# Feed-forward of a two-layer decoder: operand sums of the down projection formed beside gate and up, and its first product taken in native fp32

## The chip, the cores and the metric

One core of a Trainium2 chip runs the whole program. The metric is the device time of one execution in microseconds (us). Before the change it is 2813.67 us, the median of three runs (2801.68 to 2820.46).

## What is computed

Two decoder layers on 1024 tokens of width 1024. Each is an attention block followed by a feed-forward block; the change touches only the second.

```python
def swiglu(h, w_gate, w_up, w_down):
    return (jax.nn.silu(h @ w_gate) * (h @ w_up)) @ w_down
...
        x = x + swiglu(rms_norm(x, f_norm), w_gate, w_up, w_down)
```

The inner width D_FF is 2816, which is 22 blocks of 128. All data are float32, transposed: a tile has 128 features on the partitions and 512 tokens (half of the sequence) in the free dimension.

## The kernel before, in words

**A pair.** The function `pair` (L252) computes two blocks of output features for both halves of the tokens, that is four results of 128x512. It does so as a 2x2 block product with seven multiplications in place of eight. Four weight blocks A11, A12, A21, A22 are loaded into `raw` tiles, four sums S1 to S4 of them are formed on GpSimd (POOL, `gadd`, L163), and on the other side stand seven operands made of the activations: X11, X21, X22 and four sums, T1 to T4 (T4 and its like are made in `xadds`, L231; T3 overwrites X12). Products have numbers 1 to 7 and are issued in the order 1, 6, 5, 7, 2, 4, 3 (`ORDER`, L28). Product 1 is A11 times X11 alone.

**A split.** Each operand is used as a rounded high part and a low part (`split`, L152): ScalarE (ACT) writes the high part, VectorE (DVE) subtracts it from the source and writes the low part. One product over one block k is then three matmuls, high times high and the two mixed ones (L288). A weight operand is split once for each pair, into a `wo` tile; an activation operand once for each chunk, into an `xo` tile (ring `b4`, 28 tiles, of which five hold running sums during the down projection).

**Gate and up.** `ffn` (L1145) runs eleven iterations i. Each has a gate pair and an up pair with four blocks k, 84 matmuls a pair. The evacuation `fu` (L1169) of the up pair multiplies the up result into the stored gate result: a DVE instruction adds bank and a partial sum, a POOL instruction multiplies; only for the result (0, 0) DVE multiplies directly. Each of the four 128x512 results is stored to `hS` in DRAM (L1177).

**Down.** Here the inner width is worked through in four chunks of 3, 3, 3 and 2 blocks k (`DOWN`, L27). For each k of a chunk `hadds` (L1152) loads two rows of `hS`, 512 KB each, and forms T1 to T4 on POOL; then seven operands are split. The first two k of the first chunk are fetched during the last gate and up pairs (`PRE`, L37). A chunk has four pairs p. The pair p = 0 goes through `kmajor` (L335): seven banks are open at once, and all seven products are done for one k before the next k, so it can start when the first k is split. Its evacuation `f` (L1213) has a POOL add and a DVE add for two thirds of the results. The pairs p = 1 to 3 go product by product and add each bank into the running sums as soon as it is complete (`plus`, L295), nine DVE adds a pair.

**What sets the order.** A scheduler orders the instructions of each engine when the program is built, from its own estimate of times; on the chip each engine then works through its list in that order. All loads and stores stand in one list, on the SP queue.

Of the kernel before, what the change touches and what calls it, by code (L numbers as in the profile page):

```python
# [9 lines left out]
F32 = mybir.dt.float32  # L10
# [23 lines left out]
LAG = 12  # L34
RLAG = 7
MOFF = 56
PRE = 2  # L37
FGT = 7
LATE = (0,)
PESQ = (0, 16)  # L40
# [87 lines left out]
class Trunk:  # L128
# [120 lines left out]
            X[n, i] = t  # L249
            self.split(t[:, 0], t[:, 1], s)  # L250

    def pair(self, w, nk, X, evac, first=None, acc=None):  # L252
        nc = self.nc
        raw = []
        for b in range(4):
# [15 lines left out]
        A = {}  # L271
        src = {1: A11, 6: S2, 5: S1, 7: S3, 2: A12, 4: A22, 3: S4}
        for n in ORDER:
            t = self.tl("hl" if first and n in ORDER[5:] else "wo", "wo", (P, 2, 4, P), F32R)
            self.split(t[:, 0, 0:nk], t[:, 1, 0:nk], src[n], -1.0 if n == 4 else 1.0)
            A[n] = t
# [7 lines left out]

        def prod(n, bank, first):
            m = 0
            for k in range(nk):
                for a, b in ((0, 0), (0, 1), (1, 0)):  # L288
                    nc.tensor.matmul(bank, A[n][:, a, k], X[n, k][:, b], start=first and m == 0,  # L289
                                     stop=m == 3 * nk - 1, skip_group_check=True)  # L290
                    m += 1
# [852 lines left out]

    def ffn(self, l, e, src, dst, nxt):  # L1145
        nc, I = self.nc, self.I
        hS = self.dr.tile([22, P, T], F32, name=f"hS{l}")
        X, rs = e["X"], e["rs"]
        wg, wu = I[f"w{l}g"], I[f"w{l}u"]
        early = []  # L1150

        def hadds(i):  # L1152
            q = []
            for k in (2 * i, 2 * i + 1):
                t = self.hl("hld", dt=F32)
                self.load(t.rearrange("p a b -> p (a b)"), hS[k])
                q.append((t[:, 0], t[:, 1]))
            return self.xadds(*q)
        for i in range(11):
            s2 = {}  # L1160

            def fg(ti, hf, bank, add):
                c = self.tl("C", "s")
                self.emul(c, bank, add, rs[hf])
                nc.scalar.activation(c, c, AF.Silu)
                self.gadd(c, c, rs[hf], ALU.mult)
                s2[ti, hf] = c

            def fu(ti, hf, bank, add):  # L1169
                s = s2[ti, hf]  # L1170
                if add is None:
                    nc.vector.tensor_tensor(s, bank, s, ALU.mult)
                else:
                    u = self.tl("T", "u")
                    nc.vector.tensor_tensor(u, bank, add, ALU.add)
                    self.gadd(s, s, u, ALU.mult)
                nc.sync.dma_start(hS[2 * i + ti, :, hf * H:(hf + 1) * H], s)  # L1177
            self.pair(wg[i], 4, X, fg, first=i == 0 and (0, 1, 2, 3))
            if i == 10:
                for k in range(PRE):  # L1180
                    early.append(hadds(k))
            self.pair(wu[i], 4, X, fu)
        acc = {}
        base = 0
        for c, nk in enumerate(DOWN):
            X = {}
            for i in range(nk):
                self.xsplit(X, i, early.pop(0) if early else hadds(base + i))
            end = c == len(DOWN) - 1
            for p in range(4):  # L1190
                got = {}

                def place(ti, hf):
                    return slice((p + 4 * ti) * P, (p + 4 * ti + 1) * P), slice(hf * H, (hf + 1) * H)

                def start(ti, hf):
                    key = (p, ti, hf)
                    if c == 0:
                        if p == 0 or (p == 1 and ti == 0):
                            acc[key] = self.tl("C", "acc")  # L1200
                        else:
                            if (p, ti, 1 - hf) not in acc:
                                acc[p, ti] = self.tl("b4", "acc2", (P, 2, H))
                            acc[key] = acc[p, ti][:, hf]
                        self.load(acc[key], src[place(ti, hf)])
                    return acc[key]

                def done(ti, hf, r):
                    if end:
                        nc.sync.dma_start(dst[place(ti, hf)], r)  # L1210
                        got[ti, hf] = r

                def f(ti, hf, bank, add):  # L1213
                    r = start(ti, hf)
                    if add is not None:
                        self.gadd(r, r, add, ALU.add)
                    nc.vector.tensor_tensor(r, bank, r, ALU.add)
                    done(ti, hf, r)
                if p == 0:
                    self.pair(I[f"w{l}d{c}"][p], nk, X, f, first=tuple(range(nk)))  # L1220
                else:
                    self.pair(I[f"w{l}d{c}"][p], nk, X, done, acc=start)
                if end and nxt is not None:
                    self.absorb(nxt, p, [[got[t, h] for h in range(2)] for t in range(2)], "hl")
            base += nk
# [140 lines left out]
```

## Time and profile before

| | |
|---|---|
| median of three runs | 2813.67 us |
| the profiled execution, its own time | 2817.3 us |
| its span, first to last instruction | 2815.5 us |
| gate and up of the second layer, even stretch | about 2150 to 2549 us |
| down of the second layer | about 2549 to 2815.5 us |
| down of the first layer | about 1175 to 1475 us, its end beside the next layer's input projection |

Times inside the span are counted from its start. PE is the matmul engine, PEld its weight loads. A busy PE row says that matmuls were in flight; their ends are modelled, so the spacing of starts is the measure of throughput. The names in a row are output<-inputs; "x" with a number is how many instructions a row holds, and what stands after "<-" in brackets is what ended the idle time before it.

### The profile page before, as it was taken

How to read it: one execution, taken by the hardware profiler on the slowest of the kernel's cores; microseconds unless marked ns; L12 is line 12 of the kernel's file. 1: busy time of each engine (PE TensorE's matmuls, PEld its weight loads, DVE VectorE, ACT ScalarE, POOL GpSimd, SP SyncE). 2: the span in 40 equal slices, each digit the busy share in tenths (PEclk: the TensorE clock that was granted, in tenths of full speed). 3: DMA queues.
4: the chain of work that ended last, by engine and by line, in shares of the span. 5: the costliest groups of instructions: out<-in, count | busy, mean ns of one | idle time of the engine just before them, and what ended most of it. 6: DMA issues, size and time to landing. Idle time of an engine off the chain costs nothing.

```text
span 2815.5 us, 35148 instructions
## 1 busy us (share of the span) xinstructions
PE 2622.2 (93%) x11422; PEld 1963.0 (70%) x11422; DVE 2179.3 (77%) x3063; ACT 1367.4 (49%) x2640; POOL 1587.7 (56%) x1355
## 2 busy tenths in 40 slices
PE   7999998997899999998999998999789999998889
PEld 3775554765678888776758866666567888886667
DVE  8777777886965555788899887999799555558987
ACT  5437775673533332343367753777544333333333
POOL 5545665135576666876565533122556666678763
PEclk9999997998999999999999999999899999999999
DMA  3466645624232222242233437666242322224222
GB/s 116 162 203 196 197 148 151 160 84 143 86 98 89 85 77 86 89 149 87 76 109 125 144 123 223 151 176 181 94 133 67 108 86 75 86 77 163 90 90 90
DMA packets 166511, 343.38 MB, mean 122 GB/s; under 512 B 20524, under 2 KB 43904, under 8 KB 166328
## 3 DMA queue, kind: packets, MB, share of 16 engines
q1 hardware_dynamic: 160888, 329.21, 37.9%
q0 software_dynamic: 5056, 11.84, 1.4%
q8 instruction: 90, 1.47, 0.2%
q14 instruction: 93, 0.76, 0.1%
q10 hardware_dynamic: 384, 0.10, 0.0%
HBM read 232.96 MB, written 108.09 MB: 121 GB/s over the span
## 4 chain that ended last, share of the span: by engine, by line
PE 63%; DVE 17%; issue 5%; ACT 5%; DMA 4%; POOL 2%; SPq 0%; DVEq 0%; ACTq 0%; POOLq 0%
PE bb L289 19%; PE bc L289 13%; PE ba L289 13%; PE O L995 5%; DVE xo L156 5%; PE St L974 4%; PE P L342 3%; DVE wo L156 3%; PE Sm L948 2%; DVE acc L298 1%; DVE R L1079 1%; DVE p L985 1%; ACT xo L155 1%; PE psu L659 1%; PE Sz L1069 1%
## 5 line engine op out<-in xcount | busy, mean ns | idle before, releaser
L289 PE MATMUL bb<-xo,wo 128*128 128x512 f32 x2970 | 746.8, 398 | 13.0 <-DVE U L323 4.6
L289 PEld LDWEIGHTS bb<-xo,wo 128*128 128x128 f32 x2970 | 560.9, 190 | 155.3 <-DVE U L323 6.6
L289 PE MATMUL ba<-xo,wo 128*128 128x512 f32 x1980 | 518.6, 406 | 38.3 <-DVE acc L298 19.8
L289 PE MATMUL bc<-xo,wo 128*128 128x512 f32 x1980 | 499.3, 398 | 11.9 <-ACT sq L409 9.4
L289 PEld LDWEIGHTS ba<-xo,wo 128*128 128x128 f32 x1980 | 381.8, 194 | 140.2 <-issue 19.1
L289 PEld LDWEIGHTS bc<-xo,wo 128*128 128x128 f32 x1980 | 373.0, 189 | 107.8 <-ACT sq L409 10.2
L155 ACT ACTIVATE wo<-S 128x512 fp32r<-128x512 f32 (+2 forms) x416 | 241.5, 586 | 413.0 <-PE bb L289 128.4
L156 DVE TENSOR_TENSOR wo<-S,wo 128x512 fp32r<-128x512 f32 (+2 forms) x416 | 381.0, 919 | 72.8 <-ACT wo L155 71.4
L165 POOL TENSOR_TENSOR S<-raw 128x512 f32<-128x512 f32 (+2 forms) x208 | 292.3, 1406 | 111.8 <-DVE wo L156 93.5
L342 PE MATMUL P<-xo,wo 128*128 128x512 f32 x966 | 270.6, 425 | 67.9 <-DVE xo L156 26.0
L995 PE MATMUL O<-p,v 128*65 128x512 f32 (+3 forms) x1152 | 302.4, 364 | 7.9 <-ACT p L984 4.2
L342 PEld LDWEIGHTS P<-xo,wo 128*128 128x128 f32 x966 | 189.7, 202 | 142.5 <-DVE xo L156 39.4
L165 POOL TENSOR_TENSOR S<-raw,S 128x512 f32<-128x512 f32 (+2 forms) x104 | 133.2, 1281 | 272.6 <-issue 153.8
L165 POOL TENSOR_TENSOR s<-s,rs 128x512 f32<-128x512 f32 x156 | 234.5, 1512 | 76.5 <-DVE wo L156 45.3
L155 ACT ACTIVATE wo<-raw 128x512 fp32r<-128x512 f32 (+2 forms) x208 | 121.8, 586 | 312.3 <-PE bb L289 187.4
L156 DVE TENSOR_TENSOR wo<-raw,wo 128x512 fp32r<-128x512 f32 (+2 forms) x208 | 197.8, 951 | 34.0 <-ACT wo L155 34.0
L995 PEld LDWEIGHTS O<-p,v 128*65 128x65 f32 x1152 | 146.9, 142 | 71.5 <-ACT p L155 11.0
L985 DVE TENSOR_TENSOR p<-E,p 128x512 fp32r<-128x512 f32 (+2 forms) x288 | 182.3, 651 | 18.3 <-ACT p L984 16.3
L981 ACT ACTIVATE E<-St 128x512 f32<-128x512 f32 (+2 forms) x288 | 147.4, 518 | 96.4 <-PE St L978 67.0
L156 DVE TENSOR_TENSOR xo<-T,xo 128x512 fp32r<-128x512 f32 x138 | 152.3, 1119 | 42.2 <-ACT xo L155 41.8
L953 DVE TENSOR_REDUCE M<-Sm 128x1 f32<-128x512 f32 (+3 forms) x288 | 152.6, 549 | 26.1 <-PE Sm L951 16.3
L165 POOL TENSOR_TENSOR S<-S,raw 128x512 f32<-128x512 f32 (+2 forms) x104 | 137.7, 1324 | 21.2 <-issue 7.7
(297 smaller groups left out, 4191.6 us busy)
## 6 DMA issues: line engine op xcount, KB each, us to landing
hS<-s SPq DMA_DIRECT2D x88, 256.0 KB
hld<-hS SPq DMA_DIRECT2D x44, 512.0 KB
raw<-in_w1in_dram SPq DMA_DIRECT2D x48, 256.0 KB
Q<-fq SPq DMA_DIRECT2D x48, 256.0 KB
K<-fk SPq DMA_DIRECT2D x48, 256.0 KB
raw<-in_w0g_dram SPq DMA_DIRECT2D x44, 256.0 KB
raw<-in_w0u_dram SPq DMA_DIRECT2D x44, 256.0 KB
raw<-in_w1g_dram SPq DMA_DIRECT2D x44, 256.0 KB
```

Source lines behind the costliest of these rows:

```text
L155: nc.scalar.activation(hi, src, AF.Copy)
L156: nc.vector.tensor_tensor(lo, src, hi.bitcast(F32), ALU.subtract)
L165: return self.nc.gpsimd.tensor_tensor(o, a, b, op)
L289: nc.tensor.matmul(bank, A[n][:, a, k], X[n, k][:, b], start=first and m == 0, stop=m == 3 * nk - 1, skip_group_check=True)
L298: nc.vector.tensor_tensor(r[ti, hf], bank, r[ti, hf], ALU.add)
L342: nc.tensor.matmul(bank[n], A[n][:, a, k], X[n, k][:, b], start=m == 0 and i == 0, stop=m == len(ks) - 1 and i == 2, skip_group_check=True)
L948: nc.tensor.matmul(S[:, 0:e1 - c0], lhs[:, i * P:(i + 1) * P], rhs[:, c0:e1], start=True, stop=not diag, skip_group_check=True)
L953: nc.vector.tensor_reduce(M[:, m:m + 1], S[:, 0:n], AX.X, ALU.max)
L974: nc.tensor.matmul(S[:, o:H], k[:, j * P:(j + 1) * P], q[:, s:(hf + 1) * H], start=m == 0, stop=m == n - 1 and not diag, skip_group_check= ...
L981: nc.scalar.activation(E[:, o:H], S[:, o:H], AF.Exp)
L985: nc.vector.tensor_tensor(pl[:, o:H], E[:, o:H], ph[:, o:H].bitcast(F32), ALU.subtract)
L995: nc.tensor.matmul(a["O"][hf][0:VW, o:H], v[:, l], p[:, o:H], start=j == 0 and m == 0, stop=last and m == 2, skip_group_check=True)
```

## The change

The four sums of the activations are now formed in the gate and up loop, once per iteration, on POOL, and all seven operands are stored: `hS` holds 11 x 7 tiles of 256 KB. Two of the three POOL multiplications of `fu` become DVE multiplications that read the bank, after an add in place in the bank.

In the down projection each operand is loaded by itself, product by product: for product 1 into half of a `b4` tile, and used as it is; for the other six into a tile of ring `T` (six tiles), from which it is split. Product 1 uses the raw weight block A11 and the loaded X11 in float32, one matmul for each k in the program where there were three. `kmajor` is no longer used in down: all four pairs take the product-by-product path with nine DVE adds. `PRE` is gone; its function is taken by the order of the loads.

```diff
-PRE = 2
+NAT = (1,)
...
         for n in ORDER:
+            if n in nat:
+                A[n] = src[n]
+                continue
             t = self.tl("hl" if first and n in ORDER[5:] else "wo", "wo", (P, 2, 4, P), F32R)
...
-            for k in range(nk):
+            for k in range(nk if n in nat else 0):
+                nc.tensor.matmul(bank, A[n][:, k], X[n, k], start=first and k == 0, stop=k == nk - 1,
+                                 skip_group_check=True)
+            for k in range(0 if n in nat else nk):
...
-        hS = self.dr.tile([22, P, T], F32, name=f"hS{l}")
+        hS = self.dr.tile([11, 7, P, H], F32, name=f"hS{l}")
...
+        def keep(i, n, t):
+            nc.sync.dma_start(hS[i, n - 1], t)
...
-                    u = self.tl("T", "u")
+                    last = (ti, hf) != (1, 1)
+                    u = bank if last else add
                     nc.vector.tensor_tensor(u, bank, add, ALU.add)
-                    self.gadd(s, s, u, ALU.mult)
-                nc.sync.dma_start(hS[2 * i + ti, :, hf * H:(hf + 1) * H], s)
+                    (nc.vector if last else nc.gpsimd).tensor_tensor(s, u, s, ALU.mult)
+                if (ti, hf) != (0, 1):
+                    keep(i, 1 + 2 * ti - ti * (1 - hf), s)
...
+            X11, X12, X21, X22 = [s2[t, h] for t in range(2) for h in range(2)]
+            T1, T2, T4 = [self.tl("T", n) for n in ("T1", "T2", "T4")]
+            self.gadd(T1, X12, X11, ALU.subtract)
+            self.gadd(T2, X22, T1, ALU.subtract)
+            self.gadd(X12, X22, X12, ALU.subtract)
+            self.gadd(T4, T2, X21, ALU.subtract)
+            for n, t in ((5, T1), (6, T2), (7, X12), (4, T4)):
+                keep(i, n, t)
...
-            for i in range(nk):
-                self.xsplit(X, i, early.pop(0) if early else hadds(base + i))
+            for n in ORDER:
+                for i in range(nk):
+                    if n in NAT:
+                        if i % 2 == 0:
+                            two = self.tl("b4", "hx2", (P, 2, H))
+                        X[n, i] = two[:, i % 2]
+                        self.load(X[n, i], hS[base + i, n - 1])
+                    else:
+                        t = self.tl("T", "hx")
+                        self.load(t, hS[base + i, n - 1])
+                        X[n, i] = self.tl("b4", "xo", (P, 2, H), F32R)
+                        self.split(X[n, i][:, 0], X[n, i][:, 1], t)
...
-                if p == 0:
-                    self.pair(I[f"w{l}d{c}"][p], nk, X, f, first=tuple(range(nk)))
-                else:
-                    self.pair(I[f"w{l}d{c}"][p], nk, X, done, acc=start)
+                self.pair(I[f"w{l}d{c}"][p], nk, X, done, acc=start, nat=NAT)
```

How the engines' lists move is seen at three places of the second layer. The first is POOL where the first chunk of down passes into the second; before, sums of activations (from `hld` tiles into T) and of weights (from `raw` tiles into S) alternate:

```order
L165 TENSOR_TENSOR S_23761<-S_23759,raw 128x384
L165 TENSOR_TENSOR T_23723<-hld 128x512
L165 TENSOR_TENSOR S_23763<-raw 128x384
L165 TENSOR_TENSOR T_23725<-hld,T_23723 128x512
L165 TENSOR_TENSOR hld<-hld 128x512
L165 TENSOR_TENSOR T_23728<-T_23725,hld 128x512
L165 TENSOR_TENSOR S_23765<-raw,S_23761 128x384
L165 TENSOR_TENSOR S_23881<-raw 128x384
L165 TENSOR_TENSOR acc<-acc,r_23788 128x512
```

After the change only the four weight sums of each pair are left there:

```order
L165 TENSOR_TENSOR S_23685<-raw 128x384
L165 TENSOR_TENSOR S_23687<-S_23685,raw 128x384
L165 TENSOR_TENSOR S_23689<-raw 128x384
L165 TENSOR_TENSOR S_23691<-raw,S_23687 128x384
L165 TENSOR_TENSOR S_23788<-raw 128x384
L165 TENSOR_TENSOR S_23790<-S_23788,raw 128x384
```

Between two pairs' weight sums no POOL instruction on activations or running sums remains in down.

The second place is PE where the second chunk passes into the third; before, seven banks P of the `kmajor` pair are filled in turns of one k, between the last products of the pair before:

```order
L289 MATMUL bb<-xo,wo 128x512 x9
L342 MATMUL P_24345<-xo,wo 128x512 x2
L342 MATMUL P_24346<-xo,wo 128x512 x2
L289 MATMUL bc<-xo,wo 128x512 x9
L342 MATMUL P_24347<-xo,wo 128x512 x2
L342 MATMUL P_24345<-xo,wo 128x512 x5
L342 MATMUL P_24350<-xo,wo 128x512 x2
L342 MATMUL P_24346<-xo,wo 128x512 x5
```

After the change the native product of the new chunk (from `hx` and `raw`, three instructions) stands there, and then whole products of nine:

```order
L295 MATMUL ba<-xo,wo 128x512 x4
L295 MATMUL bc<-xo,wo 128x512 x2
L291 MATMUL ba<-hx_24089,raw 128x512 x2
L295 MATMUL bc<-xo,wo 128x512 x7
L291 MATMUL ba<-hx_24092,raw 128x512
L295 MATMUL bb<-xo,wo 128x512 x18
L295 MATMUL bc<-xo,wo 128x512 x9
```

What PE needs first of a new chunk is an operand that has only been loaded; the first split one is needed after it.

The third place is the SP list where up passes into down; s are the results of the last iteration, acc the running sums. Before, four of the six rows of the first chunk that are loaded late stand after the last stores:

```order
L1177 DMA hS_19844<-s 128x512
L168 DMA acc_23349<-x_104 128x512 x2
L168 DMA acc<-x_104 128x512
L168 DMA acc_23468<-x_104 128x512 x2
L168 DMA acc_23473<-x_104 128x512 x2
L168 DMA acc_23586<-x_104 128x512 x2
L168 DMA acc_23591<-x_104 128x512 x2
L168 DMA hld<-hS_19844 128x1024 x4
```

After the change the loads of the operands of the first chunk that are split (hx) stand between the stores of the sums of the last iteration (T_23037 is its T1, T_23038 its T2, T_23039 its T4; s is T3, in the place of X12):

```order
L1158 DMA hS_19741<-T_23037 128x512
L168 DMA hx<-hS_19741 128x512 x2
L1158 DMA hS_19741<-T_23038 128x512
L168 DMA hx<-hS_19741 128x512 x2
L1158 DMA hS_19741<-s 128x512
L168 DMA acc<-x_104 128x512
L1158 DMA hS_19741<-T_23039 128x512
L168 DMA hx<-hS_19741 128x512 x2
```

The first split operand of down is now fetched only when the first POOL sum of the last up pair is done, since the queue is worked off in order.

## Rows read from the trace of the kernel before

**Rows 1.** The page: busy time of each engine, share of the span.

```profile
PE 2622.2 (93%) x11422; PEld 1963.0 (70%) x11422; DVE 2179.3 (77%) x3063; ACT 1367.4 (49%) x2640; POOL 1587.7 (56%) x1355
```

**Rows 2.** Busy time by stretch: us, PE, PEld, DVE, ACT, POOL, clock, DMA, GB/s.

```profile
1175.00:1220.00 45.00, 38.56 (x148) 29.65 (x148) 37.49 (x51) 17.98 (x36) 31.74 (x24) 0.92 0.56 187
1220.00:1390.00 170.00, 156.04 (x637) 122.69 (x636) 154.34 (x211) 66.37 (x130) 110.50 (x82) 0.96 0.28 91
1390.00:1475.00 85.00, 80.30 (x313) 53.61 (x312) 81.39 (x113) 53.01 (x102) 52.81 (x41) 1.00 0.31 98
...
2549.00:2600.00 51.00, 43.99 (x170) 33.31 (x168) 42.60 (x56) 19.68 (x39) 37.67 (x28) 0.93 0.57 201
2600.00:2740.00 140.00, 123.18 (x503) 96.48 (x504) 128.48 (x171) 51.74 (x101) 96.00 (x71) 0.96 0.29 91
2740.00:2815.60 75.60, 70.90 (x304) 56.73 (x302) 58.90 (x107) 23.80 (x52) 24.23 (x25) 1.00 0.24 84
```

**Rows 3.** The same view for five iterations of gate and up.

```profile
2250.00:2446.00 196.00, 196.00 (x842) 157.66 (x841) 105.18 (x131) 60.62 (x101) 130.66 (x90) 1.00 0.27 81
```

**Rows 4.** Waits of PE in 2549 to 2815.6: total us, times, longest us.

```profile
PE ba L289 <- DVE acc L298: 11.3, 4, 4.9
PE P L342 <- DVE wo L156: 8.3, 6, 2.1
```

**Rows 5.** Timeline of PE at 119 us: start, us, engine, line.

```profile
118.72 0.85 PE L289 MATMUL bb<-xo,wo 128*128 128x512 f32 x3
119.41 1.02 PE L492 MATMUL psn<-sqf,oner 128*128 128x512 f32 x2
119.87 1.25 PE L289 MATMUL bb<-xo,wo 128*128 128x512 f32 x3
```

**Rows 6.** DVE groups in 2600 to 2740: busy us, mean ns, idle before.

```profile
L156 DVE TENSOR_TENSOR wo<-S,wo 128x384 fp32r<-128x384 f32 x34 | 30.3, 897 | 0.9 <-ACT wo L155 0.9
L156 DVE TENSOR_TENSOR xo<-hld,xo 128x512 fp32r<-128x512 f32 x24 | 23.1, 964 | 0.0
L156 DVE TENSOR_TENSOR xo<-T,xo 128x512 fp32r<-128x512 f32 x19 | 20.1, 1060 | 2.4 <-ACT xo L155 2.4
L156 DVE TENSOR_TENSOR wo<-raw,wo 128x384 fp32r<-128x384 f32 x16 | 16.3, 1020 | 0.0
```

**Rows 7.** Timeline of DVE at 2620 us: start, us.

```profile
2620.53 0.68 DVE L156 TENSOR_TENSOR xo<-hld,xo 128x512 fp32r<-128x512 f32 x1
2621.13 0.68 DVE L298 TENSOR_TENSOR acc<-bb,acc 128x512 f32<-128x512 f32 x1
2621.73 0.54 DVE L159 SCALAR_TENSOR_TENSOR wo<-raw,wo 128x384 fp32r<-128x384 f32 x1
2622.19 0.68 DVE L156 TENSOR_TENSOR xo<-T,xo 128x512 fp32r<-128x512 f32 x1
```

**Rows 8.** POOL groups in 2600 to 2740.

```profile
L165 POOL TENSOR_TENSOR S<-raw 128x384 f32<-128x384 f32 x16 | 19.6, 1226 | 6.5 <-DVE wo L156 5.5 <-DMA raw<-in_w1d_dram 0.7
...
L165 POOL TENSOR_TENSOR S<-raw,S 128x384 f32<-128x384 f32 x9 | 11.5, 1276 | 18.3 <-DVE wo L156 10.1 <-issue 6.9 <-DMA raw<-in_w1d_dram 1.3
...
L165 POOL TENSOR_TENSOR S<-S,raw 128x384 f32<-128x384 f32 x8 | 9.8, 1219 | 1.3 <-POOL S L165 0.5 <-POOL acc L165 0.5
```

**Rows 9.** POOL groups in 2250 to 2446, gate and up.

```profile
L165 POOL TENSOR_TENSOR s<-s,rs 128x512 f32<-128x512 f32 x35 | 51.9, 1490 | 21.2 <-DVE wo L156 14.1 <-ACT s L1165 3.7 <-DVE s L358 3.4
...
L165 POOL TENSOR_TENSOR s<-s,u 128x512 f32<-128x512 f32 x15 | 23.9, 1593 | 14.4 <-DVE u L1175 14.4
```

**Rows 10.** Timelines of SP and POOL: a 512 KB load issued, and its first use.

```profile
2620.16 0.33 SPq L168 DMA_DIRECT2D hld<-hS  x1
...
2623.82 1.41 POOL L165 TENSOR_TENSOR T<-hld 128x512 f32<-128x512 f32 x1 [4.23 <-DMA hld<-hS]
```

**Rows 11.** Waits of the SP queue, 2549 to 2815.

```profile
SPq L168 <- DVE wo L156: 100.9, 24, 10.4
```

**Rows 12.** All instructions that read or write tile hld: count, min/median/max ns.

```profile
L155 ACT ACTIVATE xo<-hld x88: 613/617/637, 1162.0 to 2765.3; 128x512 fp32r<-128x512 f32 x88
```

More of the change, by code (lines that the diff above doesn't have):

```diff
@@ L250, in xsplit, with pair @@
             self.split(t[:, 0], t[:, 1], s)
-    def pair(self, w, nk, X, evac, first=None, acc=None):
+    def pair(self, w, nk, X, evac, first=None, acc=None, nat=()):
         nc = self.nc
@@ L1146, in ffn @@
         nc, I = self.nc, self.I
-        hS = self.dr.tile([22, P, T], F32, name=f"hS{l}")
+        hS = self.dr.tile([11, 7, P, H], F32, name=f"hS{l}")
         X, rs = e["X"], e["rs"]
         wg, wu = I[f"w{l}g"], I[f"w{l}u"]
[L1150 to L1158, printed above, removed]
+        def keep(i, n, t):
+            nc.sync.dma_start(hS[i, n - 1], t)
         for i in range(11):
@@ L1173, in fu @@
                 else:
-                    u = self.tl("T", "u")
+                    last = (ti, hf) != (1, 1)
+                    u = bank if last else add
                     nc.vector.tensor_tensor(u, bank, add, ALU.add)
-                    self.gadd(s, s, u, ALU.mult)
-                nc.sync.dma_start(hS[2 * i + ti, :, hf * H:(hf + 1) * H], s)
+                    (nc.vector if last else nc.gpsimd).tensor_tensor(s, u, s, ALU.mult)
+                if (ti, hf) != (0, 1):
+                    keep(i, 1 + 2 * ti - ti * (1 - hf), s)
             self.pair(wg[i], 4, X, fg, first=i == 0 and (0, 1, 2, 3))
-            if i == 10:
-                for k in range(PRE):
-                    early.append(hadds(k))
             self.pair(wu[i], 4, X, fu)
+            X11, X12, X21, X22 = [s2[t, h] for t in range(2) for h in range(2)]
[6 more added lines that the diff above has]
+                keep(i, n, t)
         acc = {}
@@ L1211, in done @@
                         got[ti, hf] = r
[L1213 to L1218, printed above, removed]
-                if p == 0:
-                    self.pair(I[f"w{l}d{c}"][p], nk, X, f, first=tuple(range(nk)))
-                else:
-                    self.pair(I[f"w{l}d{c}"][p], nk, X, done, acc=start)
+                self.pair(I[f"w{l}d{c}"][p], nk, X, done, acc=start, nat=NAT)
                 if end and nxt is not None:
```

## The prediction

> **What bounds the kernel now.** I read the page first, then the stretches, then the waits of the stretches that lose time. The page shows PE at 93% [rows 1], an average over two very different stages. In gate and up PE is busy in 196.00 of 196 us [rows 3], with 842 matmuls, so one takes 196/842 = 0.2328 us, and no wait of PE is listed there. In down PE loses. Multiplying the matmul counts by 0.2328 us gives in the second layer [rows 2]: entry, 2549 to 2600, 170 matmuls worth 39.6 us, 11.4 us lost; two passages between chunks, 2600 to 2740, 503 worth 117.1 us, 22.9 lost; the rest, 304 worth 70.8, 4.8 lost with the tail. In the first layer the entry, 1175 to 1220, loses 10.5 us, 1220 to 1390 loses 21.7. So each entry costs about 11 us and each passage 44.6/4 = 11.2 us. Part of it is idle time, part the clock, which is granted at 0.93 and 0.96 there and at 1.00 in gate and up.
>
> Whom PE waits for is DVE: for running sums to be added and for splits to be written [rows 4]. DVE is busy 128 of 140 us at the passages, POOL 96 [rows 2]. Between them lies a second loss. On an undisturbed DVE, subtractions and adds of 512 columns start 0.60 us apart, those of 384 columns 0.46 [rows 7]; their durations are then 0.68 and 0.54. But the mean split of an activation takes (23.1 + 20.1)/43 = 1.00 us and that of a weight (30.3 + 16.3)/50 = 0.93 [rows 6]. About 0.33 us of each activation split and 0.39 of each weight split is thus waiting while POOL works.
>
> **The native product.** Down has 11 blocks k, four pairs and two layers: 88 triples of matmuls become one native matmul each. The kernel has such float32 matmuls with full 128x128 weights at line 492: six in the program, twelve in the trace, so two records each. At 119.41 us the two records hold PE until 119.87, 0.46 us, against 118.72 to 119.41 for three ordinary ones [rows 5]. The gain is one matmul of three, 88 x 0.2328 = **20.5 us**.
>
> The Trainium skill has a rule against it: FP8 and Floating Point Precision, TensorE Precision Notes, says that true float32 takes four passes through the array. By that rule a native product would cost more than the three matmuls it replaces; the two records in 0.46 us disagree with it. What it would do here is the third rival.
>
> **The passages between chunks.** DVE decides here. In the two pairs about a passage (p = 3 and p = 0) it now has to do 19 of the 21 activation splits (two tiles are free earlier), 14 weight splits, 16 adds: 19 x 0.60 + 14 x 0.46 + 16 x 0.60 = 27.4 us undisturbed, with 19 x 0.33 + 14 x 0.39 = 11.7 us of blocking 39.1 us. PE needs 126 x 0.2328 = 29.3. Loss by this reckoning 9.8, measured 11.2; I keep the difference of 1.4 us for clock and latency.
>
> After the change: product 1 has no splits on either side, three `b4` tiles are free earlier, so 15 activation splits, 12 weight splits, 18 adds: 9.0 + 5.5 + 10.8 = 25.3 us. The blocking shrinks because POOL has only weight sums left, 16 a chunk at (19.6 + 11.5 + 9.8)/33 = 1.24 us [rows 8], 19.8 us of some 60 or 33%, against 96/140 = 69% now. I take it in proportion, half: 15 x 0.16 + 12 x 0.19 = 4.7 us. DVE 30.0 us, PE 120 x 0.2328 = 27.9 us, loss 2.1 + 1.4 = 3.5. Four such passages save 4 x 7.7 = **31 us**. Ends: nothing, if the order built in keeps the stalls, and 4 x 11.2 = 45 us.
>
> The passage into the last chunk (two k) costs little now and has 9 x 0.60 + 12 x 0.42 + 18 x 0.60 = 21.2 us of DVE, 3.7 of blocking, against 100 x 0.2328 = 23.3 us of PE: about 1.5 us of loss a layer, **minus 3 us**. POOL adds, r1 copies and the U sums of `kmajor` vanish; two more DVE adds a chunk are counted above.
>
> **The entry into down.** The loads of split operands stand behind the store of T1 of the last iteration on SP. After the last up product come a DVE add, a weight split, a multiplication (three times 0.6 to 0.7 us), T1 on POOL (about 1.5 us, as its like in [rows 9]), then the load: 3.66 us from issue to first use for 512 KB [rows 10], so at most that for 256 KB, then ACT 0.62 [rows 12] and DVE 0.68. That is about 8 us in which PE, its native products already done, stands still. Afterwards DVE feeds 17 splits with eight weight splits and eight adds, about 22 us, for some 81 matmuls of 18.9 us: 3 more. With a lowered clock I take 13 us against 11 now, **minus 4 us** for both layers; the ends are 5 us better and 8 us worse each. What waits behind the T1 store on SP are all further loads, the weights of the second pair among them.
>
> **Gate and up.** Per iteration of 39.2 us POOL loses two multiplications of 1.59 us [rows 9] and gains four sums of about 1.5: 26.1 us [rows 3] become 29. DVE gains two multiplications that read a bank, as the adds of 0.68 us in [rows 7] do: 21.0 become 22.4. Stores rise from four to seven a turn, 0.79 MB more. PE has no wait now, and what hides the new work is that weights are split up to five `wo` tiles ahead, and POOL idles 13 us a turn. I cost it at nothing; if the cover goes, each us of delay costs 22 us, and I keep 0 to 14 us.
>
> **The end of layer 0** runs beside the next projection with DVE busy 81 of 85 us [rows 2]: there DVE bounds, and I take back **2 us** of PE's gain.
>
> **Sum.** 20.5 + 31 - 3 - 4 - 2 = 42 us off the profiled execution's 2817.3 us (span 2815.5): **2775 us**. That execution is 3.6 us above the median of the runs, within their spread; I leave it there.
>
> **The rivals.**
> 1. *Down becomes bound by PE alone*: all four passages close, 45 in place of 31 us, and neither the last passage nor the entry costs more than now: 20.5 + 45 - 2 = 63.5, **2754 us**. For it: DVE falls to about PE's own time. Against: two pairs still carry most of the splits of a chunk.
> 2. *Each POOL sum holds a split for its whole length.* Eight sums in two pairs block 8 x 1.24 = 9.9 us in place of 4.7: DVE 35.2, loss 8.7 a passage, 10 saved in place of 31: **2796 us**. Against: now 71 POOL instructions fill 96 us in two passages, 48 us each over the chunk, and DVE shows 12 us of blocking. The Trainium skill, SBUF — State Buffer, Who interferes with whom, states such a rule: the port pair of the two engines is a lock held for the whole instruction, against DVE instructions with both inputs in SBUF.
> 3. *Native costs four passes*: 4 x 0.2328 = 0.93 against 0.70 us, 20.5 us lost in place of gained: 2775 + 41 = **2816 us**. Against: [rows 5].
> 4. *SP becomes the bound; slower.* Now 77 loads of operands a layer stand in one list with 64 weight loads, and SP waits in order for a weight tile to be split, up to 10.4 us at once [rows 11]. If one such wait stands in front of the activation loads at each of the eight entries and passages, and the six T tiles and three free `b4` tiles don't bridge it, it costs 8 x 10.4 = 83 us: 2775 + 83 = **2858 us**. It cancels the gain from 42/8 = 5.3 us each, and shows as slower by 1% from 8.8. Against: nine operands waiting on chip are worth about 7 us of DVE's work.
>
> **Chances.** My own forecast 0.50, with a range of its own from 2757 to 2797; rival 1 0.15; rival 2 0.18; rival 3 0.07; rival 4 0.10. About 1% is what a measurement of this kernel tells from no change, here 28 us, that is 2789. Below it lie rival 1 and nearly all of mine (0.47): faster 0.62. Rivals 2 and 3 and my own rest make 0.28 for the same, rival 4 makes 0.10 for slower. The range of 2747 to 2812 leaves out half of rival 1's better side, most of rival 3 and rival 4.
>
> **What would show it.** Right: in the trace after, two records of the native product spaced 0.46 us in all; POOL at about a third in the chunks; mean activation splits near 0.85 us; a passage that loses 3 to 4 us, by the same reckoning of counts times 0.2328; an idle stretch of PE of 7 to 9 us at each entry, ended by the first split; gate and up still without a wait of PE. Wrong: native records spaced 0.93 us; splits still near 1.0 us; PE waits in gate and up for weight splits behind the T sums; at the passages PE waits that end with ACT or DVE being ready right after a load lands.

## The result, and the profile after

The changed kernel takes **2783.78 us** (median of 4 runs, 2780.21 to 2785.61), the kernel before 2812.99 us beside it (4 runs, 2801.68 to 2820.46): ratio 0.9888, interval 0.9866 to 0.9909. Its profiled execution took 2784.25 us, with a span of 2782.5 us. It ran a second time among the experiments: 2782.24 us, ratio 0.9894 (0.9873 to 0.9914). So the gain is about 30 us, 1.1%, where 42 were forecast: faster, with an interval clear of 1, and by less than forecast. One term of the sum had the wrong sign.

The page after, the line that answers to [rows 1]:

```profile
PE 2617.3 (94%) x11334; PEld 1940.8 (70%) x11334; DVE 2132.8 (77%) x3069; ACT 1342.6 (48%) x2578; POOL 1449.0 (52%) x1279
```

PE has 88 records fewer and is busy only 4.9 us less. POOL lost 139 us of work and DVE 47.

To compare the feed-forward stages without counting pieces of the neighbours, take the add of U2 behind each block-by-block pair. One such pair opens each feed-forward stage, and one opens layer 1's input projection, in every kernel of this study. The timeline of DVE after, the adds that bound the two stages (start, us):

```profile
771.57 0.68 DVE L351 TENSOR_TENSOR U<-P,r 128x512 f32<-128x512 f32 x1
...
1457.54 0.69 DVE L351 TENSOR_TENSOR U<-P,r 128x512 f32<-128x512 f32 x1
...
2123.79 0.68 DVE L351 TENSOR_TENSOR U<-P,r 128x512 f32<-128x512 f32 x1
```

The same adds before:

```profile
770.72 0.68 DVE L345 TENSOR_TENSOR U<-P,r 128x512 f32<-128x512 f32 x1
...
1473.53 0.69 DVE L345 TENSOR_TENSOR U<-P,r 128x512 f32<-128x512 f32 x1
...
2144.14 0.68 DVE L345 TENSOR_TENSOR U<-P,r 128x512 f32<-128x512 f32 x1
```

From the first add to the second: 702.8 us before and 686.0 after. From the third to the span's end: 671.4 and 658.7. So feed-forward gave 16.8 + 12.7 = 29.5 us of the 33.0 by which the spans differ. The other 3.5 us lie in attention, whose code is the same. Those stretches vary from kernel to kernel by more than that (the change run again, below), so the sums of the two feed-forward stages are the sharper measure below: 1374.2 before, 1344.7 after, and 1340.9 in the second profile of the same kernel.

Busy time by stretch after, to be read against [rows 2, 3]:

```profile
2250.00:2446.00 196.00, 196.00 (x842) 157.69 (x841) 116.74 (x141) 60.65 (x101) 144.21 (x101) 1.00 0.33 101
...
2545.00:2600.00 55.00, 45.11 (x159) 31.44 (x158) 40.61 (x64) 19.72 (x37) 15.40 (x14) 0.88 0.80 273
2600.00:2740.00 140.00, 140.00 (x560) 105.12 (x559) 115.09 (x185) 54.76 (x102) 43.82 (x39) 1.00 0.43 131
2740.00:2782.50 42.50, 38.52 (x156) 29.01 (x154) 28.87 (x54) 7.95 (x19) 7.63 (x11) 0.99 0.35 124
```

PE's pace in gate and up is untouched: 842 matmuls in 196 us, as before. The passages between chunks are closed altogether: from 2600 to 2740 PE is busy for all 140 us at a granted clock of 1.00, where by counts it lost 22.9 us before. POOL is down to 43.82 us there, from 96.00. The entry got worse: granted clock 0.88, 45.11 us busy of 55.

All waits of PE from 2500 us to the end:

```profile
PE bb L295 <- ACT xo L155: 8.4, 2, 7.1
PE bc L295 <- ACT xo L155: 1.2, 1, 1.2
PE ba L295 <- DVE acc L304: 0.2, 1, 0.2
```

The groups of matmuls from 2600 to 2740 on PE, by bank (busy us, mean ns of one, idle before); those from `hx` and `raw` are native:

```profile
L295 PE MATMUL bb<-xo,wo 128*128 128x512 f32 x252 | 64.6, 402 | 0.0
L295 PE MATMUL bc<-xo,wo 128*128 128x512 f32 x173 | 45.7, 404 | 0.0
L291 PE MATMUL ba<-hx,raw 128*128 128x512 f32 x52 | 23.9, 592 | 0.0
L295 PE MATMUL ba<-xo,wo 128*128 128x512 f32 x83 | 22.0, 400 | 0.0
```

Since PE never waits in this stretch, it gives the price of a native product. 508 ordinary records take 508 x 0.2328 = 118.26 us, and the 21.74 us that remain belong to 52 native records: 0.418 us each, two to a product, **0.84 us**. Three ordinary matmuls take 0.70. So the native products cost PE 88 x 0.14 = 12 us; I had put down 20.5 gained.

### The profile page after: what moved, and what is told of

It reads as the page before. It is cut to its first block, busy times and chain, and to the rows that moved or that the text cites. A ratio compares the mean times of both kernels' runs of the same rounds, so it can differ in the third digit from the quotient of the medians.

```text
span 2782.5 us, 35212 instructions
## 1 busy us (share of the span) xinstructions
PE 2617.3 (94%) x11334; PEld 1940.8 (70%) x11334; DVE 2132.8 (77%) x3069; ACT 1342.6 (48%) x2578; POOL 1449.0 (52%) x1279
## 5 line engine op out<-in xcount | busy, mean ns | idle before, releaser
L295 PE MATMUL bb<-xo,wo 128*128 128x512 f32 x3168 | 805.5, 400 | 22.0 <-ACT xo L155 16.4
L295 PEld LDWEIGHTS bb<-xo,wo 128*128 128x128 f32 x3168 | 598.1, 190 | 180.7 <-ACT xo L155 19.9
L295 PE MATMUL bc<-xo,wo 128*128 128x512 f32 x2112 | 543.7, 402 | 14.9 <-DVE U L355 5.3
L295 PE MATMUL ba<-xo,wo 128*128 128x512 f32 x1848 | 479.0, 402 | 15.6 <-DVE res L304 8.6
L295 PEld LDWEIGHTS bc<-xo,wo 128*128 128x128 f32 x2112 | 400.9, 190 | 119.9 <-issue 8.5
L295 PEld LDWEIGHTS ba<-xo,wo 128*128 128x128 f32 x1848 | 351.5, 191 | 108.3 <-DVE res L304 9.5
L348 PE MATMUL P<-xo,wo 128*128 128x512 f32 x504 | 150.2, 440 | 50.6 <-DVE xo L156 25.5
L156 DVE TENSOR_TENSOR wo<-raw,wo 128x512 fp32r<-128x512 f32 (+2 forms) x176 | 172.8, 982 | 18.5 <-ACT wo L155 18.5
L348 PEld LDWEIGHTS P<-xo,wo 128*128 128x128 f32 x504 | 100.8, 209 | 100.4 <-DVE xo L156 38.0
L990 ACT ACTIVATE p<-St 128x512 fp32r<-128x512 f32 (+2 forms) x288 | 148.0, 524 | 1.2 <-ACT mr L965 0.7
L165 POOL TENSOR_TENSOR S<-S,raw 128x512 f32<-128x512 f32 (+2 forms) x104 | 132.6, 1275 | 22.9 <-issue 9.6
```

Of the source, the lines that this page charges most:

```text
L156: nc.vector.tensor_tensor(lo, src, hi.bitcast(F32), ALU.subtract)
L165: return self.nc.gpsimd.tensor_tensor(o, a, b, op)
L348: nc.tensor.matmul(bank[n], A[n][:, a, k], X[n, k][:, b], start=m == 0 and i == 0, stop=m == len(ks) - 1 and i == 2, skip_group_check=True)
L990: nc.scalar.activation(ph[:, o:H], S[:, o:H], AF.Exp)
```

## The experiments

A run's median stands first, then its ratio to the kernel before on the same chip with the interval, then the sum of the two feed-forward stages in its profile. The last two columns say what PE loses by counts: the length of a stretch less 0.2328 us for each ordinary record and 0.418 for each native one, so idle time and a lowered clock together. The entry is the 75 us that begin 395 us behind the add that opens a feed-forward stage, the passages (two of the three, between chunks of three k) are the 135 us after it; both layers are added up.

| run | median us | ratio | feed-forward us | lost at the entries, us | at the passages, us |
|---|---|---|---|---|---|
| the kernel before | 2810 to 2814 | 1 | 1374.2 | 24 | 44 |
| the change | 2783.78 | 0.9888 (0.9866 to 0.9909) | 1344.7 | 31 | 1 |
| the change again | 2782.24 | 0.9894 (0.9873 to 0.9914) | 1340.9 | 29 | 1 |
| sums moved only | 2806.96 | 0.9971 (0.9957 to 0.9986) | 1363.8 | 44 | 12 |
| block by block (sums, native) | 2793.97 | 0.9937 (0.9918 to 0.9955) | 1353.0 | 35 | 1 |
| all split (sums, order) | 2791.47 | 0.9931 (0.9915 to 0.9948) | 1350.8 | 36 | 11 |
| two native products | 2798.0 | 0.9946 (0.9928 to 0.9964) | 1351.6 | 28 | 2 |
| POOL additions back | 2799.78 | 0.9958 (0.9941 to 0.9975) | 1357.5 | 39 | 7 |
| early entry | 2779.69 | 0.9874 (0.9851 to 0.9896) | 1338.8 | 24 | 1 |
| early entry, all split | 2791.43 | 0.9924 (0.9901 to 0.9947) | 1349.9 | 36 | 10 |
| the same, low halves on POOL | 2786.09 | 0.9902 (0.9883 to 0.9922) | 1346.3 | 34 | 13 |
| early entry and accumulators | 2778.28 | 0.9868 (0.9854 to 0.9881) | 1332.4 | 20 | 1 |
| the same, all split, low halves on POOL | 2788.78 | 0.9914 (0.9901 to 0.9928) | 1348.4 | 37 | 11 |

**All split.** Product 1 goes through splits as the others do.

```diff
-NAT = (1,)
+NAT = ()
```

> Product 1 of the down projection is split into fp32r halves like the six others; the order by products and the stored sums stay. Theory A (a native fp32 product holds PE for about 0.84 us: in the stretch 2600 to 2740 us of the changed kernel PE never waits, and 140 us less 508 records at 0.2328 us leave 21.7 us for 52 native records, two to a product): 88 products at 0.84 against 0.70 us, so PE gets 12 us back; the added 22 operand splits and 32 weight splits (0.70 and 0.62 us each, 35 us of DVE over some 460 us of down, where DVE is 82% busy) stay beside PE, and each layer's entry waits up to 2.1 us more, as no native product covers its first splits. 2772 to 2778 us. Theory B (0.46 us a product, as predicted from rows 5): 20 us slower, 2800 us or more.

Slower than the change, by 8 us in the medians and 10 to 12 by the ratios, whose intervals don't meet; so neither theory's time came true. On PE theory A holds: the page shows PE busy 2607.5 us against 2617.3. The time came back elsewhere. Stretch 2600 to 2740 of this run:

```profile
2600.00:2740.00 140.00, 136.43 (x579) 107.94 (x579) 115.77 (x195) 61.06 (x117) 43.84 (x36) 1.00 0.43 138
```

579 matmuls are worth 134.8 us, so PE loses 5.2 us here where the change loses nothing. Of PE's waits from 2500 us on, the longest is still the one at the entry; the waits on DVE's adds are new:

```profile
PE ba L295 <- ACT xo L155: 8.1, 2, 6.9
PE bb L295 <- DVE acc L304: 3.0, 4, 0.9
```

In layer 1 the feed-forward stage comes out as with the native product (655.8 us against 658.7 and 654.5). In layer 0 it is 9 us longer (695.0 against 686.0). In each layer the passages lose over 5 us that the change doesn't lose, and the cheaper product 1 pays for them; in layer 0 the entry loses 4 us more as well, and the rest is spread over the stage.

**Two native products.**

```diff
-NAT = (1,)
+NAT = (1, 2)
```

> Product 2 (A12 by X21) goes native beside product 1; 22 operand splits and 32 weight splits fewer. Theory A (0.84 us a native product against 0.70 us for three fp32r matmuls): another 88 x 0.14 = 12 us on PE and nothing gained, since PE is not waiting for DVE there: about 2796 us. Theory B (0.46 us a product): 20 us faster, about 2764 us. If neither moves the time (2784 us), PE is not the bound of the down projection.

Theory A by the medians, to 2 us: 14 us slower than the change (7 to 11 by feed-forward). Again PE never waits from 2600 to 2740:

```profile
2600.00:2740.00 140.00, 140.00 (x512) 96.33 (x511) 103.52 (x161) 43.02 (x80) 40.65 (x38) 1.00 0.40 130
```

The groups of PE count 108 native records in it: (140 - 404 x 0.2328)/108 = 0.4255 us, 0.85 a product. The passages had nothing left to close, and so a second native product only costs.

**POOL additions back.** POOL adds a zero to the operands of four products, so that it has 88 additions of 128x512 in down again; the values stay.

```diff
                         self.load(t, hS[base + i, n - 1])
+                        if n in (6, 5, 7, 4):
+                            self.gadd(t, t, self.zi[:, 0:1].broadcast_to([P, H]), ALU.add)
```

> On each stored sum (products 6, 5, 7 and 4) POOL adds a zero of the same size before the split, so POOL does as many 128x512 additions in down as before the change (88 over both layers), while the order by products stays. Theory P (the passages between chunks closed because POOL no longer holds up DVE): the passages reopen, 5 to 8 us at each of the six, 20 us slower or more: 2804 to 2815 us, and DVE's splits of hx take some 0.9 us as before. Theory O (they closed because the products are taken one by one, so that a chunk needs its first three operands only at its start): under 6 us slower, 2784 to 2790 us, only the entries get a POOL addition (1.2 us) longer.

16 us slower than the change by the medians, 13 to 17 by feed-forward: below theory P's 20 us or more and well above theory O's 6, so neither band holds. DVE's splits from 2600 to 2740, this run (to be read against [rows 6]):

```profile
L156 DVE TENSOR_TENSOR xo<-hx,xo 128x512 fp32r<-128x512 f32 x39 | 34.0, 887 | 2.7 <-ACT xo L155 2.4
L156 DVE TENSOR_TENSOR wo<-S,wo 128x384 fp32r<-128x384 f32 x40 | 31.6, 790 | 0.9 <-ACT wo L155 0.9
```

and in the changed kernel:

```profile
L156 DVE TENSOR_TENSOR xo<-hx,xo 128x512 fp32r<-128x512 f32 x45 | 31.7, 724 | 2.7 <-ACT xo L155 2.7
...
L156 DVE TENSOR_TENSOR wo<-S,wo 128x384 fp32r<-128x384 f32 x34 | 21.0, 621 | 0.0
```

The same split on the same engine takes 0.70 us (31.7/45) with POOL at 43.82 us of work and 0.87 (34.0/39) with POOL at 84.35. So POOL's work does stretch DVE's, and the traces show how. Undisturbed, a split lasts 0.68 us (512 columns) or 0.55 (384). In the kernel before, this one meets the POOL instruction of [rows 10], which runs from 2623.82 to 2625.23:

```profile
2624.00 1.65 DVE L156 TENSOR_TENSOR wo<-S,wo 128x384 fp32r<-128x384 f32 x1
```

It ends at 2625.65, 0.42 us after POOL. Of the splits of 512 and 384 columns from 2600 to 2740, 47 of 92 in the kernel before, 19 of 88 in the change and 46 of 87 in this run last longer than undisturbed, and every one of them ends 0.55 us (512 columns) or 0.41 to 0.42 us (384) after the end of a POOL instruction. So a split that finds POOL at work is held until POOL's instruction ends: of 125 that start in the middle of one, 112 are held; of 30 in which one starts midway, none. The holds cost DVE 32.6 us in this stretch before, 7.6 in the change and 21.4 here. The adds of a bank to `acc`, which read one operand from PSUM, are not held: they last 0.67 to 0.69 us in all three.

The passages reopened only a little, though: PE is idle 1.7 us from 2600 to 2740, and by counts the four of them lose 7 us in place of 1. Another 8 to 10 lie at the two entries, where the split operands now also wait for POOL's additions.

**Block by block.** The first pair of each chunk takes its blocks one by one through all seven products, its operands loaded and split in that order.

```diff
-            for n in ORDER:
-                for i in range(nk):
+            for i in range(nk):
+                for n in ORDER:
...
+                if p == 0:
+                    self.pair(I[f"w{l}d{c}"][p], nk, X, f, first=tuple(range(nk)), nat=NAT)
+                else:
+                    self.pair(I[f"w{l}d{c}"][p], nk, X, done, acc=start, nat=NAT)
```

> Operand sums stored and product 1 native as in the changed kernel, but the first pair of each chunk goes block by block through all seven products again, with its operands loaded and split in that order, as before the change. Theory O (order): each passage waits again for the splits of a whole block, 8 to 11 us at each of the six: 2784 + 45 to 65 us, less what PE's faster rate gives back, so 2815 us or more. Theory P (POOL's relief alone closes them): 3.5 us at each as predicted or less, 2784 to 2805 us.

About 11 us slower than the change: inside theory P's band and well below theory O's. So the order has a share and is not the whole. But its share isn't at the passages, where theory O looked for it. They stay closed block by block:

```profile
2600.00:2740.00 140.00, 140.00 (x558) 104.79 (x557) 113.29 (x176) 51.72 (x97) 56.77 (x47) 1.00 0.42 133
```

By counts 4 to 6 of the 11 us lie at the entries (35 against 29 to 31). Whether the move of the sums alone is the rest, the next run tells.

**Sums moved only.** The run before with `NAT = ()`: of the change only the move of the sums is left, with what it brings along (the operands loaded one by one, two multiplications of `fu` on DVE, no `PRE`).

> Only the move of the sums: formed beside gate and up and stored; the first pair of each chunk block by block, all products split, as before the change. Theory P (POOL's relief of DVE closes the passages, order and native product add nothing): within 4 us of the all-split run, 2790 to 2796 us. Theory of three shares (the run block by block is 12 us above the changed kernel, the all-split run 9 us above it, and the two add up): about 2803 us, 9 us below the kernel before.

The three shares hold to 4 us (2803 expected, 2806.96 measured), and theory P alone falls. With the ratios: moving the sums takes 0.29% off; the order takes another 0.40 (0.9971 to 0.9931), the native product another 0.34 (0.9971 to 0.9937). Together they make 1.03%, against 1.06 to 1.12 measured for the whole change. Of 30 us that is about 8 for the sums, 11 for the order, 10 for the native product, each to some 4 to 6 us by the intervals. Where the shares lie, the counts tell. With the sums moved, the stretch of the two passages is

```profile
2600.00:2740.00 140.00, 135.14 (x571) 107.81 (x570) 118.00 (x188) 56.56 (x107) 54.90 (x45) 0.99 0.43 134
```

571 records are worth 132.9 us, so 7.1 us are lost in place of 22.9. Over both layers the move of the sums alone takes the passages from 44 to 12 us, but the entries rise from 24 to 44, and so only 8 us are left of it. The order then gives 8 us back at the entries and 1 at the passages; the native product gives 9 at the entries and 11 at the passages, and costs PE 12.

**The change again.**

> The changed kernel itself a second time, beside the following runs. If the stretches that the change doesn't touch (0 to 778 us and 1441 to 2131 us in its first profile) come out with other lengths, differences of that size between kernels there are execution noise and not the change's doing: 2780 to 2790 us, with up to 8 us of difference in these two stretches.

The medians of the two sets agree to 1.5 us. The first attention stretch, up to the pair that opens layer 0's output projection, was 673.9 us in the first profile and 676.6 in the second; over all kernels it ran from 667.3 to 677.9, though it has the same code in all. A difference of a few us between two profiles is read in feed-forward alone, or not at all.

**Early entry.** The timeline of PE in the changed kernel at the entry into down of layer 1:

```profile
2536.32 3.60 PE L291 MATMUL ba<-hx,raw 128*128 128x512 f32 x8
2539.35 3.35 PE L295 MATMUL bb<-xo,wo 128*128 128x512 f32 x12
2542.54 2.96 PE L295 MATMUL bc<-xo,wo 128*128 128x512 f32 x12
2552.61 1.95 PE L295 MATMUL bb<-xo,wo 128*128 128x512 f32 x3 [7.11 <-ACT xo L155]
2555.81 2.38 PE L295 MATMUL bb<-xo,wo 128*128 128x512 f32 x4 [1.25 <-ACT xo L155]
```

and of its SP queue:

```profile
2548.66 0.33 SPq L1158 DMA_DIRECT2D hS<-T  x1
2549.04 0.91 SPq L168 DMA_DIRECT2D hx<-hS  x2
```

The native matmuls are done by 2540, before the last two products of up. Then PE stands still until the first split operand comes. Its load was issued at 2549.04, right behind T1's store, though what it fetches was stored long before. The experiment loads the first operands of products 6 and 5 before the last up pair and moves the last four stores of sums back:

```diff
+            if i == 10:
+                pre.update({(n, j): fetch(j, n) for n in rest[:2] for j in range(DOWN[0])})
             self.pair(wu[i], 4, X, fu)
...
-            for n, t in ((5, T1), (6, T2), (7, X12), (4, T4)):
-                keep(i, n, t)
+            late = [(i, n, t) for n, t in ((5, T1), (6, T2), (7, X12), (4, T4))]
+            if i < 10:
+                for x in late:
+                    keep(*x)
```

> The first two split products' operands of the first chunk (6 and 5) are loaded before the last up pair, the native product's operand loads and product 6's splits come in the middle of that pair, and the last iteration's four stores of sums go behind the loads of product 7. Theory (SP's order makes the entry: loads behind the stores of sums that are computed late): the 7.1 us idle before product 6 and the two waits of 1.2 us behind it go in both layers, and the clock doesn't fall: 16 to 20 us less than the changed kernel. Rival (the splits on ACT and DVE behind the last pair's evacuations set the entry): 3 to 5 us less in all.

Only 2.6 us came, a little less than even the rival had. Products 6 and 5 of the first pair now run before up is done, and PE stops later:

```profile
2554.32 1.62 PE L295 MATMUL ba<-xo,wo 128*128 128x512 f32 x3 [6.56 <-DVE acc L304]
```

Bank ba with split operands is product 2, which goes into the bank of product 1; PE waits until DVE has added that bank into its third accumulator. Accumulators and the next operands are also loaded behind a late store, and right before the add DVE has three splits to do, which take 3.48 us where POOL holds them. The wait moved on; how much of it is the loads and how much the splits, as the rival says, this run doesn't show.

**Early entry, all split**, with `NAT = ()`.

> As the entry experiment, with product 1 split like the others (products 1 and 6 loaded early). From the all-split run: PE 12 us shorter than with native products, DVE's waits (3.0 to 3.3 us a layer of bb behind DVE, and the like) stay, the 7 us at the entry go: some 15 us below the all-split run, within 4 us of the entry experiment. If DVE sets the passages now, it is slower than the entry experiment by 5 us or more.

12 us slower than its neighbour: the case in which DVE sets the passages, but not that alone. By counts the passages lose 10 us in place of 1 and the entries 36 in place of 24: the 7 us at the entry did not go (7.3 us, in front of bank bc, until ACT's first split). So the native product is worth something at both places.

**The same, low halves of product 3's operands on POOL.**

> As the run before, with the low half of product 3's operands formed on POOL (22 subtractions of 128x512) and not on DVE, which has 15 us less to do. Theory DVE-bound (PE's waits behind DVE in the all-split run come from DVE's load): 4 to 8 us faster than the run before. Theory P (POOL's work holds DVE up, as in the run with POOL's additions): no gain, 0 to 6 us slower.

5.3 us faster by the medians and 3.6 by feed-forward, with intervals that overlap: the size of the first theory, and probably more than chance. Its mechanism is borne out only in part. In layer 1 PE's waits on DVE fall from 5.5 us to 1.5, but those on ACT and POOL grow by as much, and DVE as a whole is as busy as in the run before (2163.5 against 2161.4 us), since POOL holds its splits for 18 us longer over the span. What gave the 5 us stays open.

**Early entry and accumulators.**

```diff
+        for tag, ti, hf in (("U3", 1, 1), ("r1", 1, 0), ("U2", 0, 1)):
+            acc[0, ti, hf] = self.tl(tag, "acc")
+            self.load(acc[0, ti, hf], src[4 * ti * P:(4 * ti + 1) * P, hf * H:(hf + 1) * H])
```

> As the entry experiment; in addition product 7's first operands are loaded before the last up pair (into free tiles), and the first pair's accumulators lie in tiles that the up pairs leave free, so that their loads don't wait for the stores of that pair's results. The entry experiment's idle of 7.1 and 6.6 us stood in front of product 7, whose operands and third accumulator were loaded behind a store of a late sum on SP. Theory (SP's order at the entry): both go, each layer's feed-forward is 6 us shorter than in the entry experiment, about 2766 us. Rival (ACT's and DVE's splits set the entry, 0.63 and 0.70 us each behind the last pair's evacuations): an idle of 3 us or more stays and 3 us a layer come back at most, 2773 us or more.

The long idle is gone. What remains from 2500 us on is short and belongs almost all to DVE:

```profile
PE bb L295 <- DVE wo L156: 2.3, 2, 1.9
PE bb L295 <- DVE acc L304: 1.6, 1, 1.6
PE ba L295 <- DVE xo L156: 1.3, 2, 0.9
PE bc L295 <- DVE xo L156: 0.7, 1, 0.7
PE bb L295 <- ACT wo L155: 0.7, 1, 0.7
PE ba L295 <- DVE acc L304: 0.5, 1, 0.5
```

These waits still add up to 7.1 us, against 8.2 with the early entry alone (6.9 on an add of DVE, 1.3 on ACT). What came back is the clock. The 60 us from the last products of up on, with the early entry and then with the accumulators too:

```profile
2521.00:2581.00 60.00, 51.85 (x188) 36.49 (x187) 43.17 (x64) 19.26 (x36) 25.97 (x21) 0.94 0.71 241
...
2530.00:2590.00 60.00, 52.77 (x199) 36.23 (x198) 47.74 (x69) 19.10 (x36) 25.53 (x21) 1.00 0.70 232
```

The granted clock, between its levels of 1.2 and 2.4 GHz, fell to 0.94 of the upper one over the stretch with an idle of 6.56 us in it, and stayed at 1.00 with idles of 1.9 us at most. PE does 11 records more in the same time. Operands and accumulators were moved together, so which of them dissolved the long idle isn't shown.

Feed-forward is 1332.4 us, 6.3 less than with the early entry alone, half of what the theory wanted. Its median is 2778.28 us, and its ratio of 0.9868 lies below the change's 0.9894, with intervals that overlap: better than the kernel before for certain, better than the change by some 4 us in the medians probably, and no better than the early entry alone as far as the times show. In its profile the second attention stretch was 8 us longer than in the early-entry run (573.9 against 565.9), which hides the gain in that execution; why, is open.

**The same, all split, low halves on POOL.**

> As the run before with product 1 split and the low half of product 3's operands formed on POOL. PE has 12 us less to do than with native products, DVE 20 us more. Theory (DVE binds the passages without native products): 4 to 8 us slower than the run before, as the third run of the entry set was against its first. Rival (only the entry hid the gain): 8 to 12 us faster than the run before.

10 us slower than the run before, more than the 4 to 8 of the theory; the rival falls. The entries lose 37 us here and 20 in the run before, the passages 11 and 1: moving the loads forward doesn't help the entry of the all-split form, where ACT and DVE have product 1's splits to do as well.

## Why the prediction was right or wrong

**The native product: wrong, and this is the step that failed.** The prediction says "At 119.41 us the two records hold PE until 119.87, 0.46 us". That is true of the start of the next row and not of PE's time. The price appears one row later, and [rows 5] ended one row too early. The row that follows there:

```profile
120.96 2.25 PE L289 MATMUL ba<-xo,wo 128*128 128x512 f32 x9
```

From 119.41 to 120.96 pass 1.55 us; three ordinary matmuls are 0.70 of that, so the native product takes 0.85. After the change the same shows in a block of six records:

```profile
2589.75 2.73 PE L291 MATMUL ba<-hx,raw 128*128 128x512 f32 x6
2591.92 2.18 PE L295 MATMUL bc<-xo,wo 128*128 128x512 f32 x7
2593.94 4.35 PE L295 MATMUL bb<-xo,wo 128*128 128x512 f32 x18
```

4.19 us less 7 x 0.2328 leaves 2.56 for three products, 0.85 each. Rival 3 had the sign, with a price a little high (0.93). The term forecast as 20.5 us gained is 12 us lost. The Trainium skill's rule (FP8 and Floating Point Precision, TensorE Precision Notes), four passes for true float32, is borne out in sign; four times 0.2328 would be 0.93, and the runs show 0.84 to 0.85.

Rival 3's time of 2816 us did not follow, because a second part of the forecast was wrong in the other direction. The native product frees DVE and ACT of 54 splits, and that is worth more than PE pays: with sums and order kept, taking it away costs 8 to 12 us (all split), and it costs 11.7 with the early entry as well. I had credited the splits in the reckoning of the passages, but against a PE that I thought 20 us faster. That the whole still came out 9 us from the forecast of 2775 is partly luck: the native term, 33 us too good, and the passages, some 17 too bad, lean against each other, and nothing in the prediction said that they would.

**The passages: right in mechanism, too small in size.** Forecast 11.2 to 3.5 us each; measured 0. In the change's layer 0 they lose nothing either. The DVE side came out as reckoned: with splits at 0.70 and (21.0 + 8.0)/43 = 0.67 us (the second group is weights split from `raw`, 9 at 8.0 us in the same view), blocking is 0.10 and 0.21 us where 0.16 and 0.19 were assumed, so 25.3 + 4.0 = 29.3 us for two pairs. PE's side was the error: 108 x 0.2328 + 6 x 0.84 = 30.2 us, not 27.9. PE is the longer, by 0.9 us, so it waits for nobody, as rival 1 said of the passages. The runs agree: with the sums alone the four passages lose 12 us, near the forecast's 14, and the native product closes the rest in either order. Rival 2 had the mechanism of a single hold right, since each held split waits for the end of the POOL instruction; what it had wrong is how many are held and for how long. It let each of eight sums block DVE for its whole 1.24 us, 9.9 us for two pairs; measured are 4.0, since over half of the splits meet no POOL instruction and the held ones meet one that is partly over.

In layer 1 the ledger is: stalls before, 11.4 + 22.9 + 4.8 = 39.1 us; after, 55 - (147 x 0.2328 + 12 x 0.418) = 15.8 at the entry, 0, and 4.0 in the rest; native products 44 x 0.14 = 6.1. So 39.1 - 19.8 - 6.1 = 13.2 us, against 12.7 between the marks. The forecast had 22 a layer: its native term was 16 off, the passages with the short last one 10 too low, the entry 2 too good. These are figures of one profile; in the second profile of the same kernel the stage of layer 1 is 4 us shorter.

**The entry: right, a little too small.** An idle of 7.11 us in layer 1, ended by the first ACT split behind T1's store and the load, where about 8 was forecast. With what follows and the clock the entry loses 15.8 us, forecast 13, before 11.4. That the loads of split operands stand behind the store of T1 is only a part of the cause: when the first loads were issued earlier, nearly the same idle stood a product further, and it took the accumulators and product 7's operands as well to dissolve it. The forecast lumped the clock in; the runs show it as a price of its own, paid with the long idle and not with several short ones.

**Gate and up: right.** PE's only wait from 2140 to 2530 us is 1.2 us, on a U sum of DVE, as before. POOL's 144.21 us of 196 are hidden.

**The end of layer 0: not seen.** Layer 0's stage gained 16.8 us and layer 1's 12.7 (second profile 16.5 and 16.9), so nothing shows the 2 us given back; no run singles out this end.

**SP's order as a new bound (rival 4): wrong.** SP waits a lot, but none of its waits reaches PE after the entry: from 2600 us on PE has no wait at all, and in layer 0 the 2.5 us after the entry end with DVE.

## What to carry to other kernels

The price of an instruction on a pipelined engine is read from a stretch without idle time, by counts over its whole length; the distance to the next row's start can leave the price to a later row. An instruction that is dearer on the busiest engine can still pay if it relieves the engine that this one waits for, once and no further: the first native product gave about 10 us, the second took 7 to 14. A gain in one place is to be counted in the others too: moving the sums won 32 us at the passages and lost 20 of them at the entries, where the operands came late. Where an engine stands still behind a late load, look two products ahead before moving that load, since the next one can take over the wait.

## What the runs showed of the hardware

A native fp32 matmul of 128x128 weights by 512 columns leaves two records in the trace, each shown with 0.59 us, and takes 0.84 to 0.85 us of PE (three stretches: 52, 108 and 6 records). A DVE subtraction of 512 columns with both operands in SBUF starts every 0.60 us when undisturbed. If it meets a POOL instruction, it is held until that one ends, and ends itself 0.55 us later (39 of 39 held ones from 2600 to 2740 in the kernel before, the change and the run with POOL's additions). On average it took 0.70 us in the change, 0.87 with POOL's additions and 1.00 before, with POOL busy 43.82, 84.35 and 96.00 of 140 us; but POOL's busy time alone doesn't set the average, since with two native products it was 0.78 (26.6/34) at 40.65 us. A DVE add with one operand in a bank took 0.67 to 0.69 us in all of these.
